# Graph attention on one core: a small early copy of the sorted keys, a block load in three parts, and six fewer filler products

## The chip, the core and the metric

The kernel runs on one core of one Trainium2 chip. The metric is the device time in microseconds (us) of one execution. Five engines work side by side: PE (TensorE), DVE (VectorE), ACT (ScalarE), POOL (GpSimd) and SP (SyncE), which here only issues transfers. Each engine runs its own instructions in the order in which they were written, and waits on semaphores for the others. Transfers between the chip's main memory (DRAM) and the core's memory are carried out by 16 DMA engines.

## What is computed

A graph attention layer: 4096 nodes with 64 features, 50000 edges with random ends, 4 heads of 64 outputs. Cut to what matters:

```python
x_proj[h] = x @ weight[h]
score[h, e] = (x_proj[h, src[e]] * att_src[h]).sum() + (x_proj[h, dst[e]] * att_dst[h]).sum()
score = np.where(score > 0, score, 0.2 * score)
output[h, dst[e]] += np.exp(score[h, e]) * x_proj[h, src[e]]      # over all edges
output[h, n] /= sum(exp(score[h, e]) for edges e with dst[e] == n) + 1e-8
```

The result is a 4096 x 256 float32 array, one row per node.

## The kernel before

The edges are brought into an order in which they can be gathered by one-hot products on PE. A key holds source and destination of an edge. DVE sorts the keys in two stages with min and max networks. After the first stage the sorted runs are stored to DRAM and fetched again, cut by source (the tile `raw`). The second stage, in `group`, sorts these by destination. Its result, the tile `ki` (128 x 512 integers), is stored to DRAM as `skey2` (the page calls it `gat_sorted`), and the class `Windows` fetches from it: POOL issues four indirect transfers of 128 rows x 128 keys, one for each group of eight blocks (`win[:, 0]` to `win[:, 3]`). There are 32 blocks of 128 destination nodes.

`Windows.unpack(i)` splits the keys of a group into node numbers (tiles `t`, then `tb` in bf16), with four DVE instructions for group 0 and two on DVE and two on POOL for the others, and SP stores `tb` to DRAM as `gat_bins`. `Blocks.load(b)` then reads the bins of one block back with every partition getting the same 8 KB (`bc`, 1 MB written). The buffers of `bc` are four. `onehot` compares `bc` with each partition's own number (tile `oh`), on DVE. `gather(b, c)` multiplies `oh` by the node tables on PE, in three chunks c of 6, 6 and 4 tiles (`CH`), each into one of two PSUM buffers `ps`, and ACT empties it with an exponential (`ex`) and a copy (`xs`). `weights` and `values`, or `product` by chunks, form on DVE the weights `wv` and the weighted rows `val`. `sums(b, -1)` adds up the weights on PE, `sums(b, 0)` and `sums(b, 1)` the weighted rows. The class `Finish` takes, projects, inverts and stores a block's result.

Blocks 0 and 1 don't wait for a load: `spread` copies their bins to all partitions with products by an identity matrix on PE, and ACT (for the last chunk of block 1, DVE) copies these from PSUM to `bc`. Block 0's keys come from the sorted tile itself, block 1's from `win.tb`, that is from `unpack(0)`. From block 2 on the bins come by `load`.

The order of the instructions is written by hand (the schedule is manual): each engine's queue is the order of the calls. After `group`, the main program runs one-hots and gathers of block 0, `unpack(0)`, the loads of blocks 2 to 4, the spread of block 1, and then `blocks.run(1, ...)`, a loop over blocks whose body for block b issues `load(b + 4)`, `values(b)`, the gather of block b + 1, the one-hots of block b + 2 and the sums of block b. In this loop each of ten small DVE instructions (`checks`, which find out whether an edge count was exceeded) is given to one block, and `unpack(1)`, `unpack(2)` and `unpack(3)` come at the ends of blocks 1, 4 and 8.

`busy(n)` issues n products of 512 columns on PE whose result nobody reads ("fillers", `warm`): 38 of them while the second sort ends, 7 more before block 1's spread.

## Time and profile before

| what | us |
|---|---|
| median of 3 runs | 278.76 (278.58 to 279.06) |
| the profiled execution | 279.73 |
| its span, first to last instruction | 277.9 |
| DVE busy | 250.2 (90% of the span) |
| PE busy | 205.9 (74%) |
| ACT busy | 186.1 (67%) |

The profile counts from the start of its span, and 1.83 us of the profiled execution lie outside it. The first sort takes the span up to about 57 us. A store and a fetch follow, then the second sort up to 108.5 us, a stretch in which blocks 0 and 1 get under way, and from about 127 us the loop over blocks, up to about 265 us. In the rows further down, the number in square brackets at the end is idle time just ahead of an instruction with what ended it. L numbers are lines of the kernel before.

### The profile page before, as it was taken

To read this page: it belongs to the slowest core of one execution; us is meant where nothing else is said; L and a number is where in the kernel's file an instruction comes from. 1 tells how busy PE (TensorE), PEld (TensorE's weight loads), DVE (VectorE), ACT (ScalarE), POOL (GpSimd) and SP (SyncE) were. 2 spreads that over 40 slices of the span, in tenths; PEclk is the share of its full clock that TensorE was granted. 3 is DMA by queue.
4 is the path that set the end of the run, shared out by engine and by line. 5 is a ranking of instruction groups with operands and counts; after the bars stand their busy time and mean duration, and the time that the engine had idled before them with its cause. 6 is when DMAs were issued, how large, how long until landed. Compare 5 with 4: busy or idle time off the path is not lost.

```text
span 277.9 us, 8340 instructions
## 1 busy us (share of the span) xinstructions
PE 205.9 (74%) x3455; PEld 192.8 (69%) x3455; DVE 250.2 (90%) x521; ACT 186.1 (67%) x381; POOL 42.9 (15%) x83
## 2 busy tenths in 40 slices
PE   0010799991000297689999999999999999999990
PEld 0020489991000134489999999999999999999980
DVE  5999999926999998689999999999999999999960
ACT  1970640007999705778888888888888888888850
POOL 7885000023000000703223041000000000000000
PEclk9999985555555579999999999999999999999997
DMA  3008000011000000196595856976667585765001
GB/s 115 0 6 164 2 0 2 0 47 31 0 0 0 0 2 38 45 353 277 134 360 189 352 187 228 343 277 239 253 233 290 209 296 221 288 225 174 30 32 50
DMA packets 12767, 39.57 MB, mean 142 GB/s; under 512 B 2160, under 2 KB 8496, under 8 KB 8880
## 3 DMA queue, kind: packets, MB, share of 16 engines
q1 hardware_dynamic: 10176, 36.78, 36.3%
q10 hardware_dynamic: 1840, 1.58, 2.4%
q0 software_dynamic: 704, 0.59, 1.0%
q8 instruction: 29, 0.48, 0.7%
q14 instruction: 18, 0.15, 0.2%
HBM read 33.96 MB, written 4.98 MB: 140 GB/s over the span
## 4 chain that ended last, share of the span: by engine, by line


## 5 line engine op out<-in xcount | busy, mean ns | idle before, releaser
L551 ACT CAST xs<-ps 128x1200 bf16<-128x1200 f32 (+1 forms) x96 | 100.9, 1051 | 0.0
L570 DVE TENSOR_TENSOR val<-xs,wv 128x4096 bf16<-128x4096 bf16 (+3 forms) x35 | 71.0, 2037 | 0.3 <-ACT xs L551 0.2
L614 PE MATMUL acc<-xs,val 128*128 128x128 bf16 x992 | 60.7, 219 | 0.1
L543 PE MATMUL ps<-adb,oh 128*128 128x136 bf16 x512 | 59.5, 223 | 0.0
L541 PE MATMUL ps<-xa,oh 128*128 128x72 bf16 x512 | 56.9, 196 | 2.0 <-ACT bc L508 1.1
L614 PEld LDWEIGHTS <-val 128*128 128x128 bf16 x1024 | 57.8, 98 | 0.6 <-DVE val L570 0.5
L543 PEld LDWEIGHTS <-oh 128*128 128x128 bf16 x512 | 47.5, 98 | 1.7 <-issue 1.6
L541 PEld LDWEIGHTS <-oh 128*128 128x128 bf16 x512 | 45.5, 98 | 1.0 <-DVE oh L520 0.9
L520 DVE TENSOR_SCALAR oh<-bc,pF 128x4096 bf16<-128x4096 bf16 (+2 forms) x36 | 41.1, 1141 | 3.1 <-ACT bc L508 2.4
L304 PE MATMUL cnt_ps<-sgn,sel 128*128 128x17 f32 (+1 forms) x10 | 2.5, 379 | 51.3 <-issue 31.9
L304 PEld LDWEIGHTS cnt_ps<-sgn,sel 128*128 128x128 f32 x10 | 2.3, 324 | 51.3 <-issue 51.3
L549 ACT ACTIVATE ex<-ps 128x96 bf16<-128x96 f32 (+1 forms) x96 | 24.2, 252 | 20.0 <-PE ps L547 19.8
L212 DVE TENSOR_TENSOR sA<-sB 128x256 f32<-128x256 f32 (+3 forms) x102 | 35.4, 388 | 1.5
L212 DVE TENSOR_TENSOR sB<-sA 128x256 f32<-128x256 f32 (+3 forms) x100 | 34.8, 389 | 1.5
L547 PE MATMUL ps<-xa,oh 128*128 128x72 bf16 x512 | 32.3, 197 | 0.0
L446 PEld LDWEIGHTS at_ps<-uv,xT 64*128 64x128 f32 x128 | 26.0, 314 | 0.2 <-issue 0.2
L446 PE MATMUL at_ps<-uv,xT 64*128 64x4 f32 x128 | 26.1, 341 | 0.0
L547 PEld LDWEIGHTS <-oh 128*128 128x128 bf16 x512 | 25.5, 99 | 0.1
L522 DVE TENSOR_SCALAR oh<-bc,pF 128x2048 bf16<-128x2048 bf16 (+2 forms) x36 | 24.9, 691 | 0.0
L294 ACT ACTIVATE junk<-kr,nb 128x512 f32<-128x512 f32 x32 | 23.1, 722 | 1.1
L687 PE MATMUL pf<-Wbd,aT 128*128 128x128 f32 x124 | 21.2, 293 | 0.5 <-ACT aT L675 0.5
L602 PEld LDWEIGHTS <-xs 128*128 128x128 bf16 x512 | 18.0, 96 | 0.4
(145 smaller groups left out, 244.4 us busy)
## 6 DMA issues: line engine op xcount, KB each, us to landing
bc<-gat_bins SPq DMA_DIRECT2D x30, 1024.0 KB, 5.9
out_dram<-res SPq DMA_DIRECT2D x31, 128.0 KB, 3.1
eD<-in_edge_index_dram ACTq DMA_DIRECT2D x2, 195.0 KB, 4.0
eS<-in_edge_index_dram SPq DMA_DIRECT2D x2, 195.0 KB, 3.7
gat_sorted<-sA SPq DMA_DIRECT2D x1, 256.0 KB, 2.0
gat_sorted<-ki SPq DMA_DIRECT2D x1, 256.0 KB, 2.0
gat_bins<-tb SPq DMA_DIRECT2D x4, 64.0 KB, 1.8
attbd<-in_att_src_dram POOLq DMA_DIRECT2D x4, 0.2 KB
```

The costliest lines, as they stand in the source:

```text
L212: V.tensor_tensor(out=av(d[:], at + o, [2 * h, n], [1, h]), in0=av(s[:], at, [2 * h, n], [1, h]), in1=av(s[:], at + h, [2 * h, n], [1, h]) ...
L294: S.activation(out=junk[:], in_=v, func=ACTF.Sign, bias=nbnd[:, b:b + 1], scale=1.0, accum_out=sgn[:, b:b + 1])
L446: T.matmul(out=ps[:, b, :], lhsT=nodes(b), rhs=uv[:, k, :], start=(b == 0), stop=True, skip_group_check=True)
L520: V.tensor_scalar(out=oh[:, e], in0=bc[:, e], scalar1=pF[:, 0:1], scalar2=None, op0=OP.is_equal)
L522: V.tensor_scalar(out=av(oh[:], (2 * NT + t0) * W2, [W2, nt], [1, W2]), in0=av(bc[:], (2 * t0 + 1) * W2, [2 * W2, nt], [1, W2]), scalar1=p ...
L541: T.matmul(out=ps[:, i, P:P + XC], lhsT=hot(2 * t + 1), rhs=xa[:, 2 * t, :], start=(i % 2 == 0), stop=False, skip_group_check=True)
L543: T.matmul(out=ps[:, i, 0:S0], lhsT=hot(2 * t), rhs=adb[:, b, :], start=False, stop=False, skip_group_check=True)
L547: T.matmul(out=ps[:, i, P:P + XC], lhsT=hot(2 * NT + t), rhs=xa[:, 2 * t + 1, :], start=False, stop=True, skip_group_check=True)
L549: S.activation(out=av(ex[:], 2 * t0, [2, n], [2 * NT, 2 * H], [1, 2]), in_=av(ps[:], P, [PW, n], [1, 2 * H], [0, 2]), func=ACTF.Exp)
L551: S.copy(out=xs[:, t0:t0 + n, 0:P + XC], in_=ps[:, 0:n, 0:P + XC])
L570: V.tensor_tensor(out=av(val[:], h * Dout + t * C, [Dout, nh], [C, n], [1, Din]), in0=av(xs[:], S0 + t * XW, [0, nh], [XW, n], [1, Din]), ...
L614: T.matmul(out=self.to[k], lhsT=val[:, t, k * P:(k + 1) * P], rhs=xs[:, t, 0:BD], start=apart and t == 0, stop=(t == NT - 1), skip_group_c ...
```

## The change

- The rows of `ki` that hold the first four blocks' keys (one partition in eight, 16 rows of 2 KB) are stored first, into a DRAM tensor of their own, `near2`. The whole of `ki` is stored after it, as before.
- `Windows` gets a fetch ahead of its four: 64 rows from `near2` into a tile `close`, with starting points that POOL works out.
- `unpack(0)` is split in two: partitions 0 to 63 (blocks 0 to 3) from `close`, ahead of block 0's second chunk of products, and partitions 64 to 127 from `win`, after block 1's first one-hots. Each half has its own store to `gat_bins`.
- Block 2's load is issued in three transfers, by the chunks of `CH`, and its one-hots in three parts. Block 1's weights and values are formed by `product`, in three parts that alternate with these one-hots. Block 4's load is issued after the second half of `unpack(0)`.
- The last chunk of block 1's spread is copied by ACT instead of DVE.
- The first four of the ten small `checks` stand ahead of block 0's products. The loop gets the other six.
- `unpack(1)`, `(2)`, `(3)` move from the ends of blocks 1, 4, 8 to those of 2, 6, 10.
- 32 fillers instead of 38.

```diff
@@ def group
         if between:
-            busy(38)
+            busy(32)
-        store(skey2, so.runs(RUN, ki, FINE, [lambda keys: st.count(), *(between or (quiet, quiet)),
-                                        *(lambda keys, f=f: f() for f in st.steps(0))]))
+        so.runs(RUN, ki, FINE, [lambda keys: st.count(), *(between or (quiet, quiet)),
+                                *(lambda keys, f=f: f() for f in st.steps(0))])
+        if between:
+            nc.sync.dma_start(out=near2[0, 0:NR * L].rearrange("(g e) -> g e", g=NR),
+                              in_=ki[:].rearrange("(g r) e -> g r e", g=NR)[:, 0])
+        store(skey2, ki)
@@ class Windows
+            self.close = self.win
+            if close:
+                self.close = pool.tile([NEAR, 1, W2], I32, name="close")
+                at = pool.tile([NEAR, 1], I32, name="close_at")
+                G.tensor_scalar(out=at[:], in0=start[0:NEAR, 0:1], scalar1=near[:, 0:1],
+                                scalar2=most_near[:, 0:1], op0=OP.add, op1=OP.min)
+                fetch(pool, near2, at[:], W2, self.close[:, 0], 2)
...
-        def unpack(self, i):
-            t, tb = self.t[:, i], self.tb[:, i]
+        def unpack(self, i, p0=0, p1=P):
+            t, tb = self.t[p0:p1, i], self.tb[p0:p1, i]
+            win = (self.close if p1 == NEAR else self.win)[p0:p1, i]
@@ def load
-                nc.sync.dma_start(out=t[:], in_=dataclasses.replace(bin_dram[b], ap=[[0, P], [1, 2 * NT * W2]]))
+                for t0, n in parts:
+                    nc.sync.dma_start(out=t[:, t0 * PW:(t0 + n) * PW],
+                                      in_=dataclasses.replace(bin_dram[b], offset=bin_dram[b].offset + t0 * PW,
+                                                              ap=[[0, P], [1, n * PW]]))
@@ def run
-                self.values(b, 2 if b == ND - 1 else 1)
+                if b not in self.val:
+                    self.values(b, 2 if b == ND - 1 else 1)
@@ the main program
-        win = Windows(cst, stretches.to[0][:])
+        win = Windows(cst, stretches.to[0][:], True)
...
-        for c in range(2):
+        checks = stretches.rest() + excess(so2)
+        for f in checks[:4]:
+            f()
+        blocks.product(0, 0)
+        win.unpack(0, 0, NEAR)
+        for b in (2, 3):
+            blocks.load(b, CH if b == 2 else ((0, NT),))
+        for c in (1, 2):
             blocks.product(0, c)
-        win.unpack(0)
-        for b in range(2, 5):
-            blocks.load(b)
-        blocks.product(0, 2)
         for c in range(len(CH)):
-            blocks.spread(1, c, win.tb[:, 0], lambda t: NT + t, S.copy if c < 2 else V.tensor_copy)
-            if c == 1:
-                blocks.onehot(1, *CH[0])
-        for c in (1, 2):
+            blocks.spread(1, c, win.tb[0:NEAR, 0], lambda t: NT + t, S.copy)
             blocks.onehot(1, *CH[c])
+            if c == 0:
+                win.unpack(0, NEAR, P)
+                blocks.load(4)
...
-        blocks.onehot(2)
-        blocks.weights(1)
-
-        blocks.run(1, {b: lambda i=i: win.unpack(i) for b, i in ((1, 1), (4, 2), (8, 3))},
-                   stretches.rest() + excess(so2))
+        for c in range(len(CH)):
+            blocks.onehot(2, *CH[c])
+            blocks.product(1, c)
+
+        blocks.run(1, {b: lambda i=i: win.unpack(i) for b, i in ((2, 1), (6, 2), (10, 3))},
+                   checks[4:])
```

Left out are the constants `near` and `most_near` (two small POOL instructions at the start) and the slice of the identity matrix in `spread`.

The order on SP, from the store of `ki` on, before:

```order
L286 DMA gat_sorted<-ki 128x512
L473 DMA gat_bins<-tb 128x256
L496 DMA bc<-gat_bins 128x4096 x4
L701 DMA out_dram<-res 64x2x256
L473 DMA gat_bins<-tb 128x256
```

and of the change, where lines have moved by some twenty:

```order
L414 DMA gat_near<-ki 16x512
L293 DMA gat_sorted<-ki 128x512
L496 DMA gat_bins<-tb 64x256
L516 DMA bc<-gat_bins 128x1536 x2
L516 DMA bc<-gat_bins 128x1024
L516 DMA bc<-gat_bins 128x4096
L496 DMA gat_bins<-tb 64x256
L516 DMA bc<-gat_bins 128x4096 x2
L724 DMA out_dram<-res 64x2x256
```

The store of the second half of the bins stands behind the loads of blocks 2 and 3, and the loads of blocks 4 and 5 stand behind that store.

The order on DVE from block 0's last one-hots to its last product, before (`wv` and `val` are a chunk's weights and products, `t` and `tb` the unpacking):

```order
L522 TENSOR_SCALAR oh<-bc,pF 128x512
L583 TENSOR_TENSOR wv_893<-ex 128x48
L585 TENSOR_TENSOR val<-xs,wv_893 128x4x6x64
L583 TENSOR_TENSOR wv_896<-ex 128x48
L585 TENSOR_TENSOR val<-xs,wv_896 128x4x6x64
L467 TENSOR_SCALAR t<-win 128x128
L468 TENSOR_SCALAR t<-win 128x128
L471 CAST tb<-t 128x128
L472 TENSOR_SCALAR tb<-t,boff 128x128
L583 TENSOR_TENSOR wv_910<-ex 128x32
L585 TENSOR_TENSOR val<-xs,wv_910 128x4x4x64
```

and of the change:

```order
L544 TENSOR_SCALAR oh<-bc,pF 128x512
L347 TENSOR_TENSOR pick_667<-cnt,m_158 128x32
L349 TENSOR_REDUCE sum_669<-pick_667 128x4
L350 TENSOR_SCALAR at_671<-sum_669,off_139 128x4
L352 TENSOR_SCALAR to_673<-at_671 128x4
L605 TENSOR_TENSOR wv_902<-ex 128x48
L607 TENSOR_TENSOR val<-xs,wv_902 128x4x6x64
L491 TENSOR_SCALAR t<-close 64x128
L492 TENSOR_SCALAR t<-close 64x128
L494 CAST tb<-t 64x128
L495 TENSOR_SCALAR tb<-t,boff 64x128
L605 TENSOR_TENSOR wv_916<-ex 128x48
```

The unpacking stands one chunk of products earlier, with the four checks ahead of that chunk.

The order on DVE from block 1's last one-hots to the loop's first reciprocal, before:

```order
L522 TENSOR_SCALAR oh<-bc,pF 128x512
L520 TENSOR_SCALAR oh<-bc,pF 128x4096
L522 TENSOR_SCALAR oh<-bc,pF 128x2048
L561 TENSOR_TENSOR wv<-ex 128x128
L570 TENSOR_TENSOR val<-xs,wv 128x4x16x64
L692 RECIPROCAL inv<-aT 128x4
```

and of the change, from the second part of block 2's one-hots on:

```order
L607 TENSOR_TENSOR val<-xs,wv_1074 128x4x6x64
L542 TENSOR_SCALAR oh<-bc,pF 128x1536
L544 TENSOR_SCALAR oh<-bc,pF 128x768
L605 TENSOR_TENSOR wv_1079<-ex 128x48
L607 TENSOR_TENSOR val<-xs,wv_1079 128x4x6x64
L542 TENSOR_SCALAR oh<-bc,pF 128x1024
L544 TENSOR_SCALAR oh<-bc,pF 128x512
L605 TENSOR_TENSOR wv_1084<-ex 128x32
L607 TENSOR_TENSOR val<-xs,wv_1084 128x4x4x64
L715 RECIPROCAL inv<-aT 128x4
```

Block 1's last weights (`wv_1084`) come after two chunks of its products and all of block 2's one-hots, where the whole of block 1's weights stood ahead of the products. On PE the order of the work is the same, and its `sums(1, -1)` still stands ahead of block 2's second gather.

## Rows read from the trace of the kernel before

**Rows 1.** Busy time by stretch: PE, PEld, DVE, ACT, POOL, then clock and DMA.

```profile
108.50:124.60 16.10, 11.79 (x188) 9.64 (x188) 11.87 (x28) 12.76 (x19) 5.02 (x4) 1.00 0.50 179
...
126.80:264.90 138.10, 137.98 (x2907) 136.92 (x2905) 137.31 (x193) 115.53 (x233) 12.60 (x6) 1.00 0.66 237
```

**Rows 2.** Timeline of DVE, 108 to 129 us: start, duration, line, operation, [idle].

```profile
108.92 0.62 DVE L520 TENSOR_SCALAR oh<-bc,pF 128x1536 bf16<-128x1536 bf16 x1 [0.33 <-ACT bc L508]
...
112.56 0.96 DVE L585 TENSOR_TENSOR val<-xs,wv 128x1536 bf16<-128x1536 bf16 x1 [0.54 <-ACT xs L551]
...
114.86 0.22 DVE L467 TENSOR_SCALAR t<-win 128x128 int32<-128x128 int32 x1
...
115.46 0.17 DVE L583 TENSOR_TENSOR wv<-ex 128x32 bf16<-128x32 bf16 x1
...
118.06 0.62 DVE L520 TENSOR_SCALAR oh<-bc,pF 128x1536 bf16<-128x1536 bf16 x1 [1.63 <-ACT bc L508]
...
118.92 1.22 DVE L508 CAST bc<-ps 128x1024 bf16<-128x1024 f32 x1
...
122.44 1.29 DVE L520 TENSOR_SCALAR oh<-bc,pF 128x4096 bf16<-128x4096 bf16 x1 [0.79 <-DMA bc<-gat_bins]
...
124.30 0.22 DVE L561 TENSOR_TENSOR wv<-ex 128x128 bf16<-128x128 bf16 x1
124.62 2.29 DVE L570 TENSOR_TENSOR val<-xs,wv 128x4096 bf16<-128x4096 bf16 x1
126.83 0.17 DVE L692 RECIPROCAL inv<-aT 128x4 f32<-128x4 f32 x1
...
128.20 0.22 DVE L561 TENSOR_TENSOR wv<-ex 128x128 bf16<-128x128 bf16 x1
```

**Rows 3.** Timeline of SP's issues in the same stretch.

```profile
108.54 0.33 SPq L286 DMA_DIRECT2D gat_sorted<-ki  x1
115.57 0.32 SPq L473 DMA_DIRECT2D gat_bins<-tb  x1
117.86 4.18 SPq L496 DMA_DIRECT2D bc<-gat_bins  x4
```

**Rows 4.** Timeline of POOL: the first fetch of the windows.

```profile
111.31 1.17 POOL L387 DMA_INDIRECT win<-gat_sorted,to  x1 [46.01 <-DVE oh L522]
```

**Rows 5.** DMA issues on the page: count, size, us from issue to landing.

```profile
gat_sorted<-ki SPq DMA_DIRECT2D x1, 256.0 KB, 2.0
gat_bins<-tb SPq DMA_DIRECT2D x4, 64.0 KB, 1.8
```

**Rows 6.** The window fetches, in the same form; then the first sort's fetches.

```profile
win<-gat_sorted,to POOLq DMA_INDIRECT x4, 2.8
...
DMA to landing us min/median/max: 2.5/2.5/2.5
```

**Rows 7.** The loads of block 2 (issued 117.86) and block 3 (118.3).

```profile
bc<-gat_bins SPq DMA_DIRECT2D x1, 1024.0 KB, 4.6
...
bc<-gat_bins SPq DMA_DIRECT2D x1, 1024.0 KB, 8.0
```

**Rows 8.** Timeline of PE: last fillers, spreads of blocks 0 and 1, block 2's gather.

```profile
104.66 2.10 PE L779 MATMUL warm<-adb,identb 128*128 128x512 bf16 x9
106.60 1.47 PE L506 MATMUL ps<-tb,identb 128*128 128x256 bf16 x12
...
115.69 1.47 PE L506 MATMUL ps<-tb,identb 128*128 128x256 bf16 x12 [0.94 <-DVE wv L583]
...
125.60 0.19 PE L541 MATMUL ps<-xa,oh 128*128 128x72 bf16 x1
```

**Rows 9.** Timeline of ACT: block 0's bins, block 1's copies, block 2's last exponential.

```profile
105.49 0.41 ACT L792 CAST tb<-t 128x256 bf16<-128x256 int32 x1 [9.94 <-DVE t L791]
...
116.58 2.78 ACT L508 CAST bc<-ps 128x1536 bf16<-128x1536 f32 x2 [1.79 <-issue]
...
127.72 0.25 ACT L549 ACTIVATE ex<-ps 128x64 bf16<-128x64 f32 x1
```

More of the change, by code (lines that the diff above doesn't have):

```diff
@@ L26 @@
 RUN1 = 4
+NEAR = 64
 SETS = RUN // RUN1 * 2
@@ L138 @@
     G.tensor_scalar(out=off2[:], in0=pm16[:], scalar1=float(RL), scalar2=None, op0=OP.mult)
+    near = cst.tile([NEAR, 1], F32)
+    G.tensor_scalar(out=near[:], in0=pm16[0:NEAR], scalar1=float(L - RL), scalar2=None, op0=OP.mult)
+    most_near = cst.tile([NEAR, 1], F32)
+    G.tensor_scalar(out=most_near[:], in0=pm16[0:NEAR], scalar1=float(L), scalar2=float(L - W2), op0=OP.mult,
+                    op1=OP.add)
     boff = cst.tile([P, NI], F32)
@@ L491, in __init__, with load @@
             self.bc, self.oh, self.ex, self.xs, self.wv, self.val = ({} for _ in range(6))
[L493 removed]
+        def load(self, b, parts=((0, NT),)):
             if b < ND:
                 t = self.bcp.tile([P, 2 * NT * W2], BF16, name="bc")
[L496 removed]
+                for t0, n in parts:
+                    nc.sync.dma_start(out=t[:, t0 * PW:(t0 + n) * PW],
+                                      in_=dataclasses.replace(bin_dram[b], offset=bin_dram[b].offset + t0 * PW,
+                                                              ap=[[0, P], [1, n * PW]]))
                 self.bc[b] = t
@@ L505, in spread @@
             for i in range(n):
-                T.matmul(out=ps[:, i, :], lhsT=av(identb[:], row(t0 + i), [0, P]), rhs=tb, start=(i % 2 == 0),
+                T.matmul(out=ps[:, i, :], lhsT=av(identb[0:tb.shape[0]], row(t0 + i), [0, P]), rhs=tb, start=(i % 2 == 0),
                          stop=True, skip_group_check=True)
```

27 lines of the change are left out of this document (13 added, 14 removed).

## The prediction

> **What bounds the kernel now.** I read the busy time by stretch first, then the timelines of DVE, SP, POOL, PE and ACT where a stretch has holes. In the loop, 126.8 to 264.9 us, PE is busy 137.98 of 138.10 us and DVE 137.31 [rows 1]. PE has nothing to give there and DVE next to nothing, so time that is lost or won ahead of the loop stays lost or won at the end. Between the sort and the loop, 108.5 to 124.6, DVE is busy only 11.87 of 16.10 us [rows 1]: 4.2 us of holes are the most that any reordering can win. The largest: 0.33 us until block 0's bins are copied, 0.54 until its gather is out of PSUM, 1.63 until block 1's bins are spread, 0.79 until block 2's load lands [rows 2]. The last two hang on one chain: the store of the sorted keys is issued at 108.54 [rows 3], POOL can fetch at 111.31 [rows 4], the unpacking starts at 114.86 [rows 2], the bins are stored at 115.57 and loaded from 117.86 [rows 3], and block 2's load lands 4.6 us later [rows 7], at 122.4, where DVE starts on it [rows 2]. PE's granted clock is 1.00 all through [rows 1], its upper level of 2.4 GHz.
>
> **Six fewer fillers.** Nine fillers start at 104.66, and the spread of block 0 follows at 106.60 [rows 8]: 0.22 us each, so six fewer end near 105.3. Block 0's bins are ready at 105.49 + 0.41 = 105.90 [rows 9], and the spread can start at 105.95, 0.65 us earlier. The 0.33 us hole goes, and block 0's one-hots, which ended at 112.56 − 0.54 − 0.17 = 111.85 (the hole, and a `wv` of 0.17 ahead of it [rows 2]), end at 111.2. PE idles 0.65 us more, a pause shorter than the 0.94 us ahead of block 1's spread [rows 8], through which the clock held. I cost this at nothing. If the clock fell to its lower level, part of PE's 11.79 busy us [rows 1] would take twice as long, and the end would be some 3 us later. I give that 2 in 100.
>
> **Four checks ahead of the products.** The trace has them only in the loop, apart from one another. Here each waits for the one ahead. The nearest row is `wv` to `val`, 124.30 to 124.62 [rows 2], so 0.2 to 0.3 us each; I take 0.95 in all. They end at 112.15, the first product starts 0.3 later (`wv` to `val`) and ends 0.9 later, at 113.35, about as before. So the fillers' gain pays for the checks, and no more. In the loop the four are worth little, since PE is full there; I take 0.05.
>
> **The early copy.** The full store landed 2.0 us after its issue [rows 5], at 110.54, and POOL began 0.77 later [rows 4]. For 32 KB the nearest row is the 64 KB stores with 1.8 [rows 5]; that gives POOL 111.1. A fetch lands 2.5 to 2.8 us after its start [rows 6]; for half the rows I take 2.5. So `close` is there at 113.6, and the unpacking starts 1.26 us earlier than at 114.86. The bounds: not before 113.35, when DVE comes free, and at the worst 114.4, if the store takes 2.3 (as the store of bins at 115.57 did before its load at 117.86 [rows 3]) and the fetch 2.8. POOL's new instruction for the starting points lies in the wait for the store. The wait for `close` holds up DVE's second chunk of products, whose data are ready at about 113.35; nothing else waits for that chunk so early.
>
> The Trainium skill, "DMA: Bandwidth & Descriptors", section "Anatomy of one DMA — SWDGE (gpsimd) path", speaks against this step: about 2.0 us of a transfer are fixed whatever its size. By it the small store lands no sooner than the 2.0 us of the full one, and this is the third case below. Its fit would also give 256 KB some 0.6 us on top of the 2.0, which the row of 2.0 for that store does not show.
>
> **From the unpacking to the loop.** Before, block 1's one-hots began 3.20 us after the unpacking (114.86 to 118.06 [rows 2], over the spread at 115.69 [rows 8] and the copy at 116.58 [rows 9]). Now that is 113.6 + 3.20 = 116.80. DVE has meanwhile unpacked (0.60, from 114.86 to 115.46 [rows 2]) and done two chunks of products, to 116.30: 0.3 for `wv` and 0.88 for `val` (0.96, of which the next instruction hides 0.08, as it does of the 2.29 between 124.62 and 126.83 [rows 2]), then 0.92 for the chunk of four tiles. It waits 0.50 instead of 1.63. After that it has no hole up to the loop, if the loads are in time:
>
> - six tiles of one-hots 0.86 (118.06 to 118.92 [rows 2]), the second unpacking 0.60 (new), six more 0.86 and four 0.70: 119.82. The copy by DVE, 1.22 busy [rows 2], is gone. ACT does it instead, after its two copies of 2.78 [rows 9] and still ahead of the gather that PE must first finish.
> - block 2's one-hots in parts, 0.86 + 0.86 + 0.70 = 2.42, where the whole took 1.86 (122.44 to 124.30), and block 1's products in parts, 1.18 + 1.18 + 0.92 = 3.28, where the whole took 2.53 (124.30 to 126.83 [rows 2]). Together 1.3 dearer. DVE reaches the reciprocal at 119.82 + 5.70 = 125.52, where it was at 126.83: 1.31 earlier.
> - the loads: SP stores the first bins 0.71 after the unpacking starts and loads 2.29 later, as before [rows 2, 3], at 116.6. The whole of block 2 took 4.6 [rows 7]; the first part is three eighths of it and I take 3.1, so it lands at 119.7, against 119.82 when DVE wants it. If the part took 4.6 as well, DVE would wait 1.4 and the gain would be gone. Parts two and three are wanted 2.0 and 4.0 later.
>
> **What is late next.** Block 1's last weights now come behind two products and all of block 2's one-hots, at 124.77, and PE needs them before block 2's second gather. That gather starts at 124.93 instead of 125.60 [rows 8], only 0.67 earlier, and block 2's last exponential ends at 127.30 instead of 127.72 + 0.25 [rows 9]. DVE wants it for block 2's weights, which it reaches 1.37 after the reciprocal (126.83 to 128.20 [rows 2]), at 126.89, and so waits until about 127.33. Of the 1.31 us some 0.44 are given back, and 0.87 remain. With the 0.05 of the checks: 0.9.
>
> The later `unpack(1)` to `(3)` cost what they cost before, a block or two later, and the loads behind them keep their distance of four blocks. I cost that at nothing.
>
> **The sum.** The profiled execution, 279.73, becomes 278.8, and its span of 277.9 becomes 277.0. The median of the runs is 0.97 below the profiled execution; the same 0.9 taken from 278.76 gives 277.9 us. About 0.2% (0.56 us) is what a measurement of this kernel can tell from no change.
>
> **The rivals.**
>
> 1. The forecast, −0.6 to −1.25 us (`close` between 113.35 and 113.95): 277.5 to 278.2.
> 2. The wait for the exponential does not come, since PE gets ahead while DVE's one-hots are in parts. Then the whole 1.31 and up to 0.25 of an earlier `close` remain: 277.2. Against it: the last weights stand behind 5 us of DVE work without a hole.
> 3. The copy is not early. The small store and its fetch take as long as the large ones, `close` lands at 114.1 to 114.4, the gain shrinks to 0.1 to 0.4 and the time is 278.4 to 278.7. For it: the stores of 64 KB and 256 KB differ by only 0.2 us [rows 5]. A first part of block 2 that lands one us late comes to the same.
> 4. Slower: the second half of the bins holds up block 4. Its store stands on SP behind the loads of blocks 2 and 3, and block 4's load behind that store. Block 3's load landed 8.0 us after 118.3 [rows 7], 8.4 after the first load's issue; now that is 116.6 + 8.4 = 125.0. If the store lands only then, block 4's load is issued at 125.1. Alone it takes 4.6 and lands at 129.7; the loop wants it at about 130.8 (block 3 at 125.6, the wait of 0.44, and one block: 29 of them fill the 138.1 us of the loop [rows 1], 4.76 each). Beyond 5.7 us it costs, beyond 6.6 the gain is gone, and with the 8.0 us of a load that shares the engines DVE waits 2.3 us: 278.76 − 0.9 + 2.3 = 280.2. For it: every load after the first took longer than 4.6. Against it: nothing large is ahead of it by then.
>
> **Chances.** The forecast 0.46, rival 2 0.10, rival 3 0.29, rival 4 with the clock 0.15. So faster by over 0.2% 0.56, within 0.2% 0.29, slower 0.15. The likeliest case by itself is 277.5 to 278.2. The range holds it, nearly all of rival 2 and all of rival 3, and the lesser forms of rival 4: 276.9 to 279.3.
>
> **What would show it.** Right: POOL's first fetch near 111.1 and the unpacking from `close` at 113.4 to 113.9; block 1's one-hots at 116.6 to 117.1; no DVE hole over 0.2 us from there to the reciprocal at about 125.5; a hole of 0.3 to 0.6 ahead of block 2's weights; then a loop as long as before. Wrong: a DVE wait for a `bc` load ahead of block 2, 3 or 4, a fetch at 111.3 or later, a clock below 1.00 after 105 us, or a loop whose period differs from before.

## The result: slower by 0.76%

| kernel | median us | lowest to highest | runs |
|---|---|---|---|
| before, on the same chip | 279.06 | 278.58 to 280.37 | 7 |
| changed | 281.43 | 280.49 to 281.73 | 7 |

The changed kernel takes 1.0076 times as long (95% interval 1.006 to 1.0091). That is above the predicted range, and on the other side: a form of rival 4 came, at a higher price than worked out. The profiled execution took 281.73 us, the slowest of the seven, with a span of 279.6. A few executions of any of these kernels take over 1.5% longer than its fastest; the ratios here and below leave them out, and so a ratio need not be the quotient of two medians.

Where the prediction looked for a gain, DVE's timeline of the changed kernel shows a small one, and behind it a loss:

```profile
113.91 0.41 DVE L491 TENSOR_SCALAR t<-close 64x128 int32<-64x128 int32 x1 [0.47 <-DMA close<-gat_near,close_at]
...
126.15 0.17 DVE L715 RECIPROCAL inv<-aT 128x4 f32<-128x4 f32 x1
126.86 1.29 DVE L542 TENSOR_SCALAR oh<-bc,pF 128x4096 bf16<-128x4096 bf16 x1 [0.54 <-PE ps L569]
...
131.59 0.17 DVE L715 RECIPROCAL inv<-aT 128x4 f32<-128x4 f32 x1
133.16 1.28 DVE L542 TENSOR_SCALAR oh<-bc,pF 128x4096 bf16<-128x4096 bf16 x1 [1.40 <-DMA bc<-gat_bins]
```

The unpacking starts at 113.91 instead of 114.86 and the reciprocal at 126.15 instead of 126.83 [rows 2], so DVE still comes 0.68 us earlier to the loop than in the profile of before (a run below shows that this profile was itself late). Then the one-hots of block 3 come 0.54 late (the row names PE, but their load lands just then, as the next rows show), and those of block 4 wait 1.40 us for their load. SP's timeline, then its longest wait (total us, times, longest), then the issues in short windows (count, size, us to landing) say why:

```profile
116.69 1.76 SPq L516 DMA_DIRECT2D bc<-gat_bins  x4
119.01 0.45 SPq L496 DMA_DIRECT2D gat_bins<-tb  x1
126.98 0.80 SPq L516 DMA_DIRECT2D bc<-gat_bins  x2
```

```profile
SPq L516 <- DMA gat_bins<-tb: 8.7, 2, 7.5
```

```profile
bc<-gat_bins SPq DMA_DIRECT2D x1, 1024.0 KB, 8.7
...
gat_bins<-tb SPq DMA_DIRECT2D x1, 32.0 KB, 7.9
...
bc<-gat_bins SPq DMA_DIRECT2D x1, 1024.0 KB, 6.1
```

Block 3's load, the last of the four issues from 116.69, goes out at about 118.0 and lands 8.7 later, at 126.7. The second half of the bins, 32 KB, is issued at 119.01 and lands 7.9 us later, at 126.9, right behind it. Only then can block 4's load go, at 126.98, and it takes 6.1. In the kernel before, the four loads stood behind one another from 117.86 to 122.04 [rows 3], and the store of all eight blocks' bins, issued at 115.57 with no load ahead of it, landed in 2.3 (1.8 is the median of four such stores [rows 5]). The Trainium skill, "DMA: Bandwidth & Descriptors", section "Queues, rings and completion order", says that on each DMA engine the descriptors of an issuing engine's queue are consumed in ring order, though they need not complete in that order. The trace agrees, the small store landing 0.2 us after the load that it stands behind.

A second thing is in no row of before. The changed kernel by stretch (busy us of PE, PEld, DVE, ACT, POOL, then the granted clock, DMA share and GB/s):

```profile
108.50:124.60 16.10, 13.07 (x184) 10.95 (x184) 14.31 (x40) 12.75 (x18) 6.38 (x6) 0.89 0.54 163
...
119.00:120.00 1.00, 1.00 (x24) 1.00 (x21) 0.98 (x3) 0.92 (x3) 0.00 (x0) 0.89 0.84 255
120.00:121.00 1.00, 1.00 (x13) 1.00 (x11) 1.00 (x3) 0.90 (x1) 0.00 (x0) 0.50 1.05 260
```

Against [rows 1], DVE is busy 14.31 of 16.10 us instead of 11.87: the holes are mostly filled, but with work that was not there before. And PE's clock falls to 0.50, the lower level of 1.2 GHz, from about 119.8 to 123.2: 13 products in the microsecond from 120 on, 24 in the one ahead of it. In the loop the clock is 1.00 again.

Third, 2.13 us of this execution lie outside the span; of before it was 1.83.

### The profile page after: what moved, and what is told of

It reads as the page before. It is cut to its first block, busy times and chain, and to the rows that moved or that the text cites. A ratio compares the mean times of both kernels' runs of the same rounds, so it can differ in the third digit from the quotient of the medians.

```text
span 279.6 us, 8350 instructions
## 1 busy us (share of the span) xinstructions
PE 205.6 (74%) x3449; PEld 192.8 (69%) x3449; DVE 251.8 (90%) x532; ACT 187.2 (67%) x382; POOL 45.4 (16%) x87
## 4 chain that ended last, share of the span: by engine, by line
## 5 line engine op out<-in xcount | busy, mean ns | idle before, releaser
L573 ACT CAST xs<-ps 128x1200 bf16<-128x1200 f32 (+1 forms) x96 | 100.8, 1050 | 0.0
L592 DVE TENSOR_TENSOR val<-xs,wv 128x4096 bf16<-128x4096 bf16 (+3 forms) x34 | 68.7, 2031 | 0.2 <-ACT xs L573 0.2
L565 PE MATMUL ps<-adb,oh 128*128 128x136 bf16 x512 | 60.5, 225 | 0.2 <-issue 0.2
L563 PE MATMUL ps<-xa,oh 128*128 128x72 bf16 x512 | 57.8, 197 | 2.2 <-DVE oh L542 0.8
L565 PEld LDWEIGHTS <-oh 128*128 128x128 bf16 x512 | 48.1, 99 | 1.4 <-issue 1.2
L563 PEld LDWEIGHTS <-oh 128*128 128x128 bf16 x512 | 46.0, 99 | 1.8 <-DVE oh L542 1.5
L569 PE MATMUL ps<-xa,oh 128*128 128x72 bf16 x512 | 32.7, 199 | 0.1
L569 PEld LDWEIGHTS <-oh 128*128 128x128 bf16 x512 | 25.8, 99 | 0.3 <-DVE oh L544 0.3
L457 PEld LDWEIGHTS at_ps<-uv,xT 64*128 64x128 f32 x128 | 24.8, 300 | 0.3 <-issue 0.3
L457 PE MATMUL at_ps<-uv,xT 64*128 64x4 f32 x128 | 24.8, 331 | 0.0
```

The lines of the kernel that those rows point to most:

```text
L457: T.matmul(out=ps[:, b, :], lhsT=nodes(b), rhs=uv[:, k, :], start=(b == 0), stop=True, skip_group_check=True)
L563: T.matmul(out=ps[:, i, P:P + XC], lhsT=hot(2 * t + 1), rhs=xa[:, 2 * t, :], start=(i % 2 == 0), stop=False, skip_group_check=True)
L565: T.matmul(out=ps[:, i, 0:S0], lhsT=hot(2 * t), rhs=adb[:, b, :], start=False, stop=False, skip_group_check=True)
L569: T.matmul(out=ps[:, i, P:P + XC], lhsT=hot(2 * NT + t), rhs=xa[:, 2 * t + 1, :], start=False, stop=True, skip_group_check=True)
L573: S.copy(out=xs[:, t0:t0 + n, 0:P + XC], in_=ps[:, 0:n, 0:P + XC])
L592: V.tensor_tensor(out=av(val[:], h * Dout + t * C, [Dout, nh], [C, n], [1, Din]), in0=av(xs[:], S0 + t * XW, [0, nh], [XW, n], [1, Din]), ...
```

## The experiments

"E1" is the changed kernel with its queue mended, and most of the others start from it. The last two columns are counts over all runs: the time outside the span, and how many runs had a mean granted clock of 0.881 or less (profiles without a fall after 105 us show 0.884 to 0.889, those with one 0.873 to 0.886, so this is a coarse sign). Over all chips the kernel before has 15 of 105 such runs.

| run | what it is | median us | ratio to before, 95% | outside span | low clock |
|---|---|---|---|---|---|
| | changed | 281.43 | 1.0076 [1.006, 1.0091] | 2.1–2.2 | 2 of 7 |
| f2 | changed, another chip | 281.14 | 1.0067 [1.0042, 1.0091] | 2.1–2.3 | 5 of 6 |
| E1 | block 3's load behind the store | 280.21 | 1.0039 [1.0018, 1.006] | 2.1–2.2 | 5 of 12 |
| e2 | changed, 38 fillers | 282.1 | 1.0085 [1.006, 1.0111] | 2.4 | 3 of 6 |
| e3 | E1, 38 fillers | 280.94 | 1.007 [1.0042, 1.0098] | 2.1–2.4 | 4 of 12 |
| e4 | before, 32 fillers | 279.21 | 0.9999 [0.998, 1.0018] | 1.8 | 1 of 12 |
| e5 | E1 without the early copy | 280.97 | 1.0069 [1.0044, 1.0094] | 2.2 | 3 of 7 |
| e6 | E1, more fillers | 280.3 | 1.0045 [1.0025, 1.0065] | 2.3–2.5 | 1 of 12 |
| e7 | E1, block 2 whole | 279.86 | 1.0024 [1.001, 1.0038] | 1.8 | 7 of 12 |
| e8 | E1, one unpacking | 279.22 | 0.9996 [0.9978, 1.0013] | 1.8 | 2 of 12 |
| g1 | e8, block 2 whole | 279.48 | 1.0001 [0.9987, 1.0014] | 1.8 | 0 of 12 |
| e9 | before, spread on 64 rows | 280.89 | 1.0015 [0.9967, 1.0064] | 1.8 | 5 of 6 |
| f3 | e9, seven fillers on 64 rows too | 282.54 | 1.0103 [1.0071, 1.0136] | 1.8 | 5 of 6 |
| e10 | E1, spread on 128 rows | 280.19 | 1.0008 [0.997, 1.0046] | 2.1–2.2 | 0 of 6 |
| f1 | changed, spread on 128 rows | 281.67 | 1.0078 [1.0049, 1.0107] | 2.1–2.3 | 0 of 6 |

**Is it the queue? E1.**

```diff
         win.unpack(0, 0, NEAR)
-        for b in (2, 3):
-            blocks.load(b, CH if b == 2 else ((0, NT),))
+        blocks.load(2, CH)
 ...
                 win.unpack(0, NEAR, P)
+                blocks.load(3)
                 blocks.load(4)
```

> One edit to the changed kernel: block 3's load is issued behind the store of the second half of the bins instead of ahead of it. Queue theory (that store, issued at 119.0 us, lands 7.9 us later because 2 MB of loads are ahead of it on the same engines, so block 4's load is issued only at 127.0 and DVE waits 1.40 us for it): with half the bytes ahead the store lands by about 123.5, block 4's load by about 129.5, the 1.40 us wait is gone, and the time falls by 1.2 to 1.6 us, to a ratio of 1.001 to 1.004 against the kernel before. Clock theory (the granted clock at 0.50 from 119.9 to 123.1 us is what costs): the time stays within 0.4 us of the changed kernel, ratio 1.006 to 1.009, and a stretch at 0.50 is still there.

Measured 280.21 us, about half of the loss gone. With only block 2's load ahead of it, the store (issued at 118.82) lands in 5.2 us instead of 7.9. That is still some 2 us after the last part of that load; block 3's load, 1 MB, is issued right behind the store. DVE's timeline of E1, where the wait for block 4 is gone and 0.29 for block 3 remains:

```profile
113.64 0.46 DVE L491 TENSOR_SCALAR t<-close 64x128 int32<-64x128 int32 x1 [0.43 <-DMA close<-gat_near,close_at]
...
117.01 0.62 DVE L542 TENSOR_SCALAR oh<-bc,pF 128x1536 bf16<-128x1536 bf16 x1 [0.43 <-issue]
...
125.98 0.17 DVE L715 RECIPROCAL inv<-aT 128x4 f32<-128x4 f32 x1
126.44 1.29 DVE L542 TENSOR_SCALAR oh<-bc,pF 128x4096 bf16<-128x4096 bf16 x1 [0.29 <-DMA bc<-gat_bins]
...
131.17 0.17 DVE L715 RECIPROCAL inv<-aT 128x4 f32<-128x4 f32 x1
```

So the wait in the queue is shown, in the rows. Its size, 1.0 us, is a difference between two chips; against f2's ratio it is 0.8. But the kernel with the queue mended is still slower than before, and no predicted gain is seen.

**Is it the fillers? e2, e3, e4.** e2 is the changed kernel and e3 is E1, each with 38 fillers; e4 is the kernel before with 32:

```diff
 # e2, e3
-            busy(32)
+            busy(38)
 # e4
-            busy(38)
+            busy(32)
```

> One edit to the changed kernel: 38 fillers again. Clock theory: PE's pause of 1.62 us ahead of block 0's spread goes, no stretch at a granted clock of 0.50 follows at 119 to 123 us, and block 2's second gather starts about 0.9 us earlier; the time falls by about 0.9 us, ratio 1.003 to 1.006. Queue theory: block 4's load is issued when the store of the bins has landed, which PE's clock doesn't touch, so the DVE wait for block 4 grows by what PE wins and the time stays within 0.4 us of the changed kernel, ratio 1.006 to 1.009.

> Both edits to the changed kernel: block 3's load behind the store of the second half of the bins, and 38 fillers. If the two causes are both real and nothing else is, this is the time that was forecast: 0.5 to 1.2 us below the kernel before, ratio 0.9955 to 0.998. If only the queue costs, the ratio is that of the first edit alone, 1.001 to 1.004; if only the clock, that of the second alone, 1.003 to 1.006.

> One edit to the kernel before: 32 fillers instead of 38. Clock theory: the longer pause of PE ahead of block 0's spread alone is enough for a stretch at 0.50 in 108 to 126 us, and the time grows by 0.5 to 2 us, ratio 1.002 to 1.007. If fewer fillers only bring the spread forward: block 0's one-hots end 0.4 to 0.65 us earlier, the clock stays at 1.00, and the time falls by 0 to 0.4 us, ratio 0.9985 to 1.000.

The clock falls with 38 fillers as with 32, so their number is not the cause of the fall. Neither run is faster for it: e3, which would have been 0.5 to 1.2 us below the kernel before if the queue and the fillers were all, is 0.7% above it, outside each of the ranges that it was given. And e4, the kernel before with the six fillers gone, is as fast as before: 0.9999. Its profile, beside that of e9 (the kernel before with 38 fillers and an edit that comes later, below), shows what was odd in the profile of before. PE's timeline, first e4, then e9:

```profile
105.92 1.47 PE L506 MATMUL ps<-tb,identb 128*128 128x256 bf16 x12 [1.25 <-ACT tb L792]
```

```profile
105.63 1.47 PE L507 MATMUL ps<-tb,identb 128*128 128x256 bf16 x12
```

With 38 fillers too the spread of block 0 mostly starts by 106.1 (105.63 in e9, 105.84 to 106.06 in four further profiles). In the profile that the prediction read, it started at 106.60 [rows 8], and the clock had risen later there, as it had in the other two late ones of the eight profiles with 38 fillers (e2 with 106.46, g2 with 106.92). With 32 it started by 106.2 in all eleven profiles, also where the clock rose that late (f2, 105.81). The stretches 99 to 101 us of the kernel before and of e9:

```profile
99.00:100.00 1.00, 1.00 (x4) 0.40 (x3) 0.97 (x3) 0.00 (x0) 0.00 (x0) 0.50 0.00 0
100.00:101.00 1.00, 1.00 (x5) 0.32 (x4) 0.97 (x4) 0.00 (x0) 0.00 (x0) 0.61 0.00 0
```

```profile
99.00:100.00 1.00, 1.00 (x5) 0.39 (x4) 0.96 (x3) 0.00 (x0) 0.00 (x0) 0.94 0.00 0
100.00:101.00 1.00, 1.00 (x6) 0.49 (x5) 0.93 (x4) 0.00 (x0) 0.00 (x0) 1.00 0.00 0
```

So the six fillers' 0.65 us are there only in executions with a late rise of the clock, three of eight here, and not in the median. What an undisturbed kernel before does is e4's timeline on DVE, here with the loop's last reciprocal:

```profile
113.96 0.26 DVE L467 TENSOR_SCALAR t<-win 128x128 int32<-128x128 int32 x1
...
117.20 0.62 DVE L520 TENSOR_SCALAR oh<-bc,pF 128x1536 bf16<-128x1536 bf16 x1 [1.63 <-ACT bc L508]
...
126.13 0.17 DVE L692 RECIPROCAL inv<-aT 128x4 f32<-128x4 f32 x1
...
131.09 0.17 DVE L692 RECIPROCAL inv<-aT 128x4 f32<-128x4 f32 x1
...
269.27 0.17 DVE L692 RECIPROCAL inv<-aT 128x4 f32<-128x4 f32 x1
```

With 38 fillers the first reciprocal is at 126.19 in e11, 126.33 in f4 and 125.65 in e9. Against e4, E1 is 0.32, 0.19 and 0.15 us early, and at the second reciprocal 0.08 late. That is less than the 0.7 by which e9 and f4 differ.

**What are the parts worth? e5, e7, e8, g1.** All start from E1. e5 has no early copy (both halves are unpacked from `win`). e7 has block 2's load, one-hots and products whole. e8 has no early copy, one unpacking and one store, and with them block 1's spread takes 128 rows again (more on this below). g1 is e8 and e7 together:

```diff
 # e5 and e8, no early copy
-        win = Windows(cst, stretches.to[0][:], True)
+        win = Windows(cst, stretches.to[0][:])
 # e7 and g1, block 2 whole
-        blocks.load(2, CH)
+        blocks.load(2)
...
-        for c in range(len(CH)):
-            blocks.onehot(2, *CH[c])
-            blocks.product(1, c)
+        blocks.onehot(2)
+        blocks.weights(1)
 # e8 and g1, one unpacking
-        win.unpack(0, 0, NEAR)
+        win.unpack(0)
...
-                win.unpack(0, NEAR, P)
```

> The kernel of the run with block 3's load behind the second bins store (280.21 us, ratio 1.0039), without the early copy: the small store and its fetch are gone, both halves of the unpacking read the full fetch, everything else stays. If the early copy is worth what its own path showed, 0.13 us at POOL and 0.3 us at the unpacking, the unpacking starts at about 114.0 and the reciprocal at 126.2 to 126.4, and the span is 0.0 to 0.3 us longer (277.6 to 277.9). Second question: 2.1 to 2.4 us lay outside the span in the four profiled kernels with the early copy, 1.8 in the two without. If its tensor and transfers cause that, it is back to 1.8 here and the time is 279.6 to 280.0 (ratio 1.001 to 1.003). If not, it stays at 2.1 or more and the time is 280.2 to 280.6 (ratio 1.004 to 1.006).

> The same kernel with block 2's load, its one-hots and block 1's weights and values whole again, as in the kernel before. By the prediction's own terms the parts cost DVE 0.56 and 0.75 us more, and save the wait until the whole load has landed. The load would be issued at 116.4 and land 4.6 later at 121.0, DVE would want it at about 120.3: a wait of 0.7, and the reciprocal at 125.98 + 0.7 - 1.3 = 125.4, 0.6 earlier than with parts: ratio 1.000 to 1.003. If the parts are worth what they were made for, the reciprocal is at 126.0 or later and the ratio is 1.004 to 1.006.

> The same kernel with the unpacking whole from the full fetch: no early copy, one unpacking instead of two halves, one bins store, the loads of blocks 2 to 4 behind one another as before. What remains of the change are the parts of block 2 and block 1, ACT's copy, the moved checks and 32 fillers. DVE loses 0.6 us of second unpacking and gets the bins some 0.3 later, in a hole that is there anyway. If DVE's added work had eaten the holes, the reciprocal comes at 125.4 to 125.8, the span is 276.8 to 277.2, 1.8 us lie outside it, and the time is 278.6 to 279.0 (ratio 0.997 to 0.9995). If the early copy carried the change, the reciprocal is at 126.2 or later and the ratio at 1.002 to 1.005.

> The run with one unpacking (279.22 us, ratio 0.9996), with block 2's load, its one-hots and block 1's weights and values whole as well. Of the change there remain the four checks ahead of block 0's products, ACT's copy of the last spread chunk, 32 fillers and the later unpackings. The load would be issued at 116.2 and land 4.6 us later at 120.8; whole one-hots and values then take 1.86 and 2.53, so the reciprocal comes at 125.2 to 125.4, against 126.13 in the kernel before with 32 fillers. If of that 0.8 about half is given back at the wait for block 2's last exponential, the time is 0.3 to 0.5 us under the kernel before: ratio 0.998 to 0.9995. If the load lands later than 121.2, the ratio is 0.9995 to 1.001.

e8 and g1 are even with the kernel before, e7 0.24% behind, and e5, at 1.0069, is above both of the ranges given for it. So what loses, beside the queue, comes with the halves (e5 loses no less without their copy), or with the spread on 64 rows that goes with them. The four checks, ACT's copy, the later unpackings and the parts of block 2 together neither gain nor lose, within some 0.2%. The early copy by itself moved little: counted from the first store's issue, the unpacking starts 5.11 us later in E1, 5.24 in e5 and 5.30 in e8. (The ratios of E1 and e5 differ by 0.3%, within their intervals.) Why nothing gains is first in a row of g1, DVE's timeline where all of block 2 is wanted at once:

```profile
121.84 1.29 DVE L539 TENSOR_SCALAR oh<-bc,pF 128x4096 bf16<-128x4096 bf16 x1 [1.66 <-DMA bc<-gat_bins]
```

At 120.18 DVE is ready for block 2, 0.61 us earlier than in e4 (where it waited 0.94 and began at 121.73), and it begins no earlier, since the load is not there: my 120.8 for its landing was a microsecond off. In parts there is no wait, but the work is dearer, and block 2's exponential is late next. e8, with the loop's last reciprocal:

```profile
125.90 0.17 DVE L712 RECIPROCAL inv<-aT 128x4 f32<-128x4 f32 x1
...
127.75 0.23 DVE L580 TENSOR_TENSOR wv<-ex 128x128 bf16<-128x128 bf16 x1 [0.43 <-ACT ex L568]
...
131.08 0.17 DVE L712 RECIPROCAL inv<-aT 128x4 f32<-128x4 f32 x1
...
269.68 0.17 DVE L712 RECIPROCAL inv<-aT 128x4 f32<-128x4 f32 x1
```

The second reciprocal, in the loop, stands at 131.09 in e4. And PE, which is full in the loop [rows 1], comes to it no earlier. It now waits for block 1's last weights ahead of block 2's second gather. PE's timeline of E1, then of e4:

```profile
125.32 0.25 PE L624 MATMUL acc<-wv,xs 128*128 128x4 bf16 x4 [0.88 <-DVE wv L605]
125.42 0.19 PE L563 MATMUL ps<-xa,oh 128*128 128x72 bf16 x1
```

```profile
124.89 0.19 PE L541 MATMUL ps<-xa,oh 128*128 128x72 bf16 x1
```

That gather starts at 125.34 to 125.56 in the four profiles with the parts and no earlier fall that reaches it (e8, E1, e10, f1). In e4, e9, e11 and f4 it starts at 124.41 to 125.09, and in g1, with block 2 whole, at 125.00. So it is the parts that hold PE up. The loop itself is not as long as before either. From the first reciprocal to the last it takes 143.1 us in e4 and in the profile of before, 143.5 in E1, 143.8 in e8 and 143.7 in g1, with DVE waiting again for exponentials (0.30 at 152.0 and 0.22 at 161.9 in e8). Which of the edits lengthens it, the later unpackings or another, no run separates.

**Is it PE's pauses, or the 64 rows? e6, e9, e10.** e6 puts fillers into the pauses of E1:

```diff
-        busy(7)
+        busy(10)
...
             blocks.onehot(1, *CH[c])
+            if c == 1:
+                busy(4)
```

> The same kernel with three more filler products ahead of block 1's spread (10 instead of 7) and four new ones behind the spread's second chunk, so that PE pauses less between 112 and 120 us. If the granted clock's fall to 0.50 at about 119 us, seen in three of five profiles of the changed family, follows from PE's pauses there, no run shows it: no run above 280.6, the mean falls to 279.8 to 280.0 and the interval becomes narrow (ratio 1.002 to 1.003). If the fall has another cause, one run in two to three stays 1 to 3 us above the fastest and the ratio stays at 1.003 to 1.006. The fillers themselves cost PE 0.6 and 0.9 us, inside pauses of about 0.9 and 1.6.

In e6's profile the clock holds to 125.5, then is 0.50 until 129, where the changed kernel's was 0.50 from 120 to 123. Only one of its 12 runs has a low mean clock, but three still took 281.4 to 282.5. Half a hit: the low clocks are fewer, but the fall in the profile has moved and not gone, and the mean is not the 279.8 to 280.0 that was expected.

In the changed family block 1's spread multiplies by 64 rows (`64*128 64x256` in its rows, `128*128 128x256` before [rows 8]). e9 makes this one edit in the kernel before, and e10 takes it back in E1:

```diff
 # e9, in the kernel before
-            blocks.spread(1, c, win.tb[:, 0], lambda t: NT + t, S.copy if c < 2 else V.tensor_copy)
+            blocks.spread(1, c, win.tb[0:NEAR, 0], lambda t: NT + t, S.copy if c < 2 else V.tensor_copy)
 # e10 (in E1) and f1 (in the changed kernel): tbn is a tile whose other 64 rows are zero
-            blocks.spread(1, c, win.tb[0:NEAR, 0], lambda t: NT + t, S.copy)
+            blocks.spread(1, c, tbn[:], lambda t: NT + t, S.copy)
```

> The kernel before with one edit: the products that spread block 1's bins take 64 rows of the array instead of 128, as in the changed kernel. The result is the same (only rows 16 to 31 carry block 1), and each product keeps its 256 columns and its duration. Theory: the half rows are why the granted clock falls to 0.50 at 117 to 120 us, which it did in five of the seven profiled kernels that spread with 64 rows and in none of the three that spread with 128. Then more than half of the runs here show a mean granted clock under 0.8855 (21 of 59 did for the kernel before), the profile if it is such a run shows the fall at 116 to 120 us, and the median is 0.4 to 1.2 us longer: ratio 1.0015 to 1.005. Rival: the falls come from pauses of PE or from chance, and the rows have no part in it: about a third of the runs under 0.8855, ratio 0.9985 to 1.0015.

> The kernel of the run with block 3's load behind the second bins store (280.21 us, ratio 1.0039, nine of twelve runs under a mean clock of 0.8855), with block 1's spread on 128 rows again: the first half is unpacked into a tile of its own whose other 64 rows are zero. No instruction that the engines wait for is added. If the half rows make the clock fall, about a third of the runs are under 0.8855, as in the kernel before, the runs above 280.6 are gone and the median is 279.6 to 279.9: ratio 1.0015 to 1.003; what then remains is mostly the 0.35 us more outside the span. If the rows have no part in it, the ratio stays at 1.003 to 1.006 with two thirds of the runs under 0.8855.

Five of e9's six runs have a low clock, none of e10's, whose ratio is a little below the range given for it. But on that chip 5 of 11 runs of the kernel before have one too, and both intervals are wide: inconclusive by themselves. Hence a larger dose (f3), and on the same chip the changed kernel itself (f2) and on 128 rows (f1):

```diff
 # f3, on top of e9
-                T.matmul(out=t[:], lhsT=identb[:], rhs=adb[:, 0:4, 0:P], start=True, stop=True)
+                T.matmul(out=t[:], lhsT=identb[0:rows], rhs=adb[0:rows, 0:4, 0:P], start=True, stop=True)
...
-        busy(7)
+        busy(7, NEAR)
```

> The kernel before with 64 rows instead of 128 in block 1's spread and in the seven fillers ahead of it: a larger dose of the same thing. Theory: more than half of the runs have a mean granted clock of 0.881 or less (five of six with the spread alone, 12 of 70 for the kernel before), and a profile of such a run shows 0.50 from some point between 113 and 120 us. Ratio 1.003 to 1.007. Rival, the rows have no part: no more such runs than in the kernel before beside it, ratio 0.9985 to 1.0015.

> The changed kernel itself, on the same chip as the one with full rows, as its control. Ratio to the kernel before about 1.0076 as measured. Under the theory of the half rows a third to a half of its runs have a mean granted clock of 0.881 or less; under the rival as few as in the kernel before (12 of 70 so far).

> The changed kernel with one thing undone: block 1's spread takes 128 rows of the array again (the first half is unpacked into a tile of its own whose other 64 rows are zero). Its second bins store still stands behind the loads, so the wait for block 4's load stays. If the half rows make the clock fall, hardly any run has a mean granted clock of 0.881 or less and the median comes 0.4 to 0.9 us below the changed kernel's on this chip. If not, both agree within 0.3 us and the shares of such runs are alike.

f3, the kernel before with 64 rows in the spread and in the seven fillers ahead of it, is 1.03% slower, more than expected. Five of its six runs have a low clock, down to 0.863, against 1 of 17 runs of the kernel before on that chip. Its profile, the mildest of its runs, from 118 to 121 us:

```profile
118.00:119.00 1.00, 0.76 (x21) 0.69 (x19) 1.00 (x2) 0.42 (x1) 0.00 (x0) 1.00 0.84 246
119.00:120.00 1.00, 1.00 (x17) 1.00 (x15) 1.00 (x4) 0.42 (x2) 0.00 (x0) 0.53 1.01 426
120.00:121.00 1.00, 1.00 (x12) 1.00 (x11) 0.71 (x3) 0.88 (x1) 0.00 (x0) 0.50 1.01 401
```

So the 64 rows make the fall more frequent: on this chip 5 of 6 runs of f3 and of f2 have a low clock, against 0 of 6 of f1 and 1 of 17 of the kernel before. They are not the only way to one: in e8's profile, on 128 rows, the clock was 0.50 from about 110.6 to 114.0. And f1, the changed kernel on 128 rows, with no fall in its profile and no low clock in any run, is not faster than f2 (281.67 and 281.14): my expectation was wrong. f1's rows show where DVE waits instead, DVE's timeline first, then SP's, then the landing of block 3's load and of the store:

```profile
125.94 0.17 DVE L717 RECIPROCAL inv<-aT 128x4 f32<-128x4 f32 x1
127.90 1.29 DVE L544 TENSOR_SCALAR oh<-bc,pF 128x4096 bf16<-128x4096 bf16 x1 [1.79 <-DMA bc<-gat_bins]
...
132.51 0.17 DVE L717 RECIPROCAL inv<-aT 128x4 f32<-128x4 f32 x1
134.07 1.28 DVE L544 TENSOR_SCALAR oh<-bc,pF 128x4096 bf16<-128x4096 bf16 x1 [1.39 <-DMA bc<-gat_bins]
```

```profile
116.47 1.75 SPq L518 DMA_DIRECT2D bc<-gat_bins  x4
118.80 0.45 SPq L498 DMA_DIRECT2D gat_bins<-tb  x1
128.03 0.80 SPq L518 DMA_DIRECT2D bc<-gat_bins  x2
```

```profile
bc<-gat_bins SPq DMA_DIRECT2D x1, 1024.0 KB, 10.0
...
gat_bins<-tb SPq DMA_DIRECT2D x1, 32.0 KB, 9.2
```

In this execution DVE waits 3.18 us for the loads of blocks 3 and 4. It is the slowest of f1's six (282.99). f2's profile, with the clock at 0.50 from about 118.1 to 121.5, is near f2's median (281.06), and its waits are shorter:

```profile
127.02 1.29 DVE L542 TENSOR_SCALAR oh<-bc,pF 128x4096 bf16<-128x4096 bf16 x1 [0.80 <-DMA bc<-gat_bins]
...
131.97 1.29 DVE L542 TENSOR_SCALAR oh<-bc,pF 128x4096 bf16<-128x4096 bf16 x1 [0.18 <-DMA bc<-gat_bins]
```

So for the same order of the queue these two waits came to 0.98, 1.94 and 3.18 us in three executions. How much of that has to do with the clock is not shown by one profile of each. On 128 rows, mending the queue is worth 1.0078 − 1.0008, some 2.0 us; on 64 rows it was 1.0076 − 1.0039, some 1.0 us. Each is a difference between two chips, with intervals too wide to tell the one from the other.

**What lies outside the span? e11, f4, g2.** In all runs of each kernel this time is nearly constant: 1.74 to 1.84 us in every run of the kernel before, 2.1 or more in the changed one. Three guesses, each added to the kernel before: 22 more POOL instructions, four more transfers on SP's queue, eleven more DVE instructions.

```diff
 # e11, behind the fetches (g2: range(11), V.memset)
+        for _ in range(22):
+            G.memset(more[:], 0.0)
 # f4, in the store of a block's output
+                for p0, p1 in (((0, 64), (64, P)) if 10 <= b < 14 else ((0, P),)):
+                    eng.dma_start(out=dst[p0 // 2:p1 // 2], in_=src[p0:p1])
```

> The kernel before with 22 more instructions that nobody waits for: memsets of one element per partition on POOL, behind its four fetches at about 118 us, where POOL is idle until 133. Outside the span lay 1.8 us in every run of the four kernels with 8328 to 8341 instructions, 2.1 to 2.2 in those with 8346 and 8350, 2.4 in those with 8362 and 8364. If the number of instructions sets it, 2.3 to 2.45 lie outside the span here (8362 instructions), the span stays at 277.1 to 277.6 and the time is 279.5 to 280.0: ratio 1.0015 to 1.003. If the number of transfers or the change's own work sets it, 1.8 remain and the ratio is 0.999 to 1.001.

> The kernel before with four more transfers on SP's queue: the outputs of blocks 10 to 13 are stored in two halves each. 8344 instructions. Outside the span lay 1.8 us in the kernels with up to two more transfers on SP's queue than the kernel before, and 2.1 to 2.4 in those with three or four. If the number of transfers sets it, 2.1 to 2.2 lie outside here, at a span of 277.1 to 277.8. If not, 1.8.

> The kernel before with eleven more DVE instructions, memsets of one element per partition right behind the sort. What lies outside the span was 1.8 us in the kernels with 520 to 528 DVE instructions and 2.1 to 2.4 in all with 532. If the length of DVE's program sets it, 2.1 to 2.2 lie outside the span here, and the span is 0.5 to 1.2 us longer because the memsets stand in DVE's way. If not, 1.8 remain outside.

All three kept 1.74 to 1.84, and e5 had shown that it is not the small copy. (Their medians: e11 280.2 in four runs, f4 279.28, g2 280.52, whose memsets stand in DVE's way.) So this third of a microsecond stays open. It is there in every kernel that has both the halves and the parts of block 2, and in none that lacks either (e7, e8, g1).

## Why the prediction was wrong

**The baseline, first.** *Six fewer fillers* failed: 0.65 us from one late execution, which the median does not have. I saw that the profiled execution stood 0.97 us above the median and still took the same 0.9 off both. The 0.97 and the 0.65 were in part one thing. e4 measured the term at 0.0 (0.9999).

**The early copy** was right in place and wrong in worth. Forecast 111.1 and 113.6; measured 111.38 and 113.91 in the changed kernel's profile, in which the sort ended 0.2 later, 111.16 and 113.64 in E1. POOL's timeline of E1, then e4's:

```profile
111.16 0.99 POOL L394 DMA_INDIRECT close<-gat_near,close_at  x1 [1.54 <-DMA gat_near<-ki]
```

```profile
111.29 0.94 POOL L387 DMA_INDIRECT win<-gat_sorted,to  x1 [46.09 <-DVE oh L522]
```

32 KB against 256 KB stored bring POOL 0.13 us, where 0.2 were forecast (111.1 against 111.31): about as little as rival 3 had said. The Trainium skill's fixed 2.0 us ("DMA: Bandwidth & Descriptors", "Anatomy of one DMA — SWDGE (gpsimd) path"), which I had weighed against this step, fits better than my row of 1.8, though it is a fit for transfers that GpSimd issues and these are SP's: in the changed kernel the small store landed in 1.9, the full one in 2.2. The 1.26 us ahead of 114.86 were mostly the late execution; against e4's 113.96 they are 0.32.

**Four checks ahead** fits: E1's first unpacking waits 0.43 for `close`, so they lie in a hole. **From the unpacking to the loop** is right as a path, 0.46 late at its end: forecast 125.52, measured 125.98 in E1 and 126.15 in the changed kernel. The first part of block 2 landed 3.7 us after its issue, where I took 3.1. But the reciprocal of an undisturbed kernel before is at 126.13, not 126.83, and so the gain of 1.31 is 0.15, less than the scatter of single executions. The two costs that I had counted, 1.3 us of dearer parts and 0.60 of second unpacking, use up the holes that they fill.

**What is late next**: the wait for the exponential came where it was put, 0.43 in e8 and e10 against 0.44, and so rival 2 is out. In the changed kernel it lies under the later one for the load. But the gather ahead of it, forecast at 124.93 and 0.67 earlier than before, started at 125.42 in E1, 0.33 behind those weights where I took 0.16, and that is 0.5 later than in e4. The loop, which I had taken to be as long as before with the later unpackings at nothing, is 0.4 to 0.6 longer in E1, e8 and g1.

**Rival 4** named the mechanism, and its price was mis-sized. I took block 3 to land at 125.0 and block 4's load to be issued at 125.1. They were 126.7 and 126.98, and in f1's profile 127.8 and 128.03: two loads begun earlier took 10.0 us (116.69 to 126.7), where the same two took 8.4 from 117.86 [rows 7]. The three parts of block 2 alone took some 6.7 of it, where the whole had taken 4.6; why, no run separates. I took block 4's load alone at 4.6, and it took 6.1, 5.9 in f1 and 4.7 in f2. I missed that block 3 itself comes late (by 0.54 here, 0.80 in f2, 1.79 in f1). At 0.15 the chance was too low for a store that I knew to stand behind 2 MB, with "nothing large is ahead of it by then" as the only reason against. That spoke of block 4's load once it is issued, and not of when the store ahead of it lands.

**The clock**: 2 in 100, for the pause behind the fillers. I had put that pause at 0.65 us and it was 1.62 (1.25 in e4), but the clock held through it. It fell behind block 1's spread, and I had not read the halved rows of that product as anything but the same 256 columns. In the changed kernel no cost of this fall could be measured (f1 against f2).

**What the loss is made of.** By the ratios, 0.76% are 2.1 us. The order of the queue is about 1.0 of it (E1; 2.0 on 128 rows, f1 and e10). The step from e8, level with the kernel before, to E1 is 1.2: 0.35 outside the span, which stays open, and 0.8 for the halves and the early copy, their clock, DVE work and block 3's wait together. These I can't divide further, since the intervals are as wide as the pieces, and so their cause stays open. The rest of the change (e8, g1) is worth nothing either way. No version beat the kernel before.

(In the sums of the prediction one term is off: the forecast's largest gain, 1.25, is 1.15 by its own bounds, 0.9 and the 0.25 to 113.35. Nothing hangs on it.)

## What to carry to other kernels

Before a term is read off one profile, ask whether that execution is above the median, and whether the term is the reason. A small store queued behind large loads landed 0.2 to 2 us after the last of them: whatever waits for it should be reckoned from that landing, not from a store's own time. Work that is split to fill a wait should be priced against the wait in an undisturbed run; here 1.9 us of added DVE work filled holes whose end was set by transfers, and the weights that it put off made PE wait.

## What the hardware showed that was not expected

- A store of 32 KB took 1.8 us or so with nothing ahead of it (SP's issue at 114.86 to the load at 116.69), and 5.2 (E1), 7.9 (the changed kernel) and 9.2 (f1) behind loads of 1, 2 and 2 MB on the same queue.
- Products on 64 rows of the array have the same duration as on 128 (1.47 us for twelve), but the granted clock fell to 0.50 behind them in eight of ten profiles, and with seven fillers on 64 rows as well the kernel was 1.03% slower. With 128 rows 20 of 168 runs of all kernels and chips had a low mean clock; with 64, fillers in the pauses (e6) apart, 39 of 74.
- The place where the clock rises differs between executions of kernels that are the same up to there: between 98 and 99 us in three profiles (f3, f4, e11), just after 99 in e9, near 100.8 in the profile of before, and between 101 and 102 in g2.
